# Accumulating transfers ordered behind the power, the convolution's mean moved one branch earlier, and the feed-forward reloads in pairs

## The chip, the cores and the metric

The kernel runs on one core of one Trainium2 chip. The metric is the device time of one execution in microseconds (us), the median of several runs. TensorE is called PE here, VectorE DVE, ScalarE ACT, GpSimd POOL and SyncE SP; each has its own queue of instructions and takes them strictly in order.

## What is computed

Two layers of a hybrid encoder over 1024 positions of 1024 channels, float32 in and out. Cut to what matters here:

```python
for l in range(2):
    h = rmsnorm(x, attn_norm_g[l])
    z = h @ w_in[l] + b_in[l]                       # 1024 -> 6912 channels
    a = zc_left * sigmoid(zc_right)                 # branch 0: convolution
    a = silu(layernorm(dwconv_causal(a, conv_w)))   #   31 taps per channel
    u, v = gelu(zg)                                 # branch 1: gated MLP
    sv = blockwise(ws, layernorm(v)) + bs           #   chunks of 128 positions
    p = multiscale_pool(zp, pool_w, pool_scale)     # branch 2: pooling
    y = g0*(a @ conv_proj) + g1*((u*sv) @ gmlp_proj) + g2*(p @ pool_proj)
    x = x + y @ w_out[l]
    h = rmsnorm(x, ffn_norm_g[l])
    h = dwconv_causal(h @ w_up[l], ffn_conv_w[l])   # 3 taps
    x = x + (gelu(h_left) * h_right) @ w_down[l]
return rmsnorm(x, final_norm_g)
```

## The kernel before

Everything lies transposed: 128 channels on the partitions, positions along the free axis, in two halves of 512. Each float32 operand of a matrix product is kept as a rounded part and a remainder, and a product of two operands is three matmuls (rounded by rounded, rounded by remainder, remainder by rounded). The weights of a product are loaded by SP (tiles `raw`, five buffers) and split on the way: ACT casts the rounded part, DVE subtracts it to get the remainder (`split`, L281 and L282), three operands ahead of their use. Of the three matmuls on one operand the first two read only ACT's part of the weights, the third reads DVE's.

The large input products (`IN_BLOCKS`: blocks `glu`, `v`, `zp`, `u`, `gate`, and the 16 `up` blocks of the feed-forward part) use a seven-product scheme over two by two blocks: a block is `first()` (two raw operands), `second()` (the sum s2) and `rest()` (s3, s1, one raw operand, s4), twelve matmuls of 128x512 to a product and half. The sums s1 to s4 of weight quarters are made by transfers: `begin` (L208) loads one quarter by SP, and `more` (L211 to L214) adds others by accumulating transfers on POOL's queue. The pool of these tiles has eight buffers (`s`), which the gate reloads `gt` and the tiles `uf` of the gated MLP use too. The first four blocks of a phase (`EARLY`) run on one half of the positions (operands `B`) while the other half is normalised, and then on the other (operands `T`).

The normalisation of a half goes through `rsqrt_sums` (L404 and on): PE sums squares (`st`), DVE makes `var` (L416), POOL raises it to the power -1/2 (`rs`, L418), DVE makes `rp` and the diagonal `dg` (L420 to L426), and PE spreads it over the partitions (`r`, L439). POOL has little else to compute; its queue is filled by the accumulating transfers, a memset of a part of `ws` that needs the load of `ws` to have landed (L527, L528), and in the feed-forward part the last three stores `hd` (L951).

Work that isn't the products' own is held by generators in a list `background`, and `pump(n)` runs n steps of it at places in the loops, with `PUMP = (1.4, 3, 5)` for the input blocks, branch 2 and branch 1: the 30 taps of each convolution tile (`conv_taps`, L583, one store of the tile to DRAM at its end, L588, and the sum `csum` of all tiles), the pooling windows, the gated MLP's spatial product (`spatial`: reloads v and u, the products `sv`, then `svf` and `us`), and `conv_norm`: it reloads `csum` and the six convolved tiles (`convn`), subtracts the mean, sums squares, then normalises and applies silu.

After the input blocks of a layer come the pooling product (`mix`, 84 matmuls in the order of the tiles, on `pooled_0` to `pooled_5`, of which the last three are reloaded at its start), branch 2 (`ph_2_k` on `mixed`), branch 1 (`ph_1_k` on `us`) and branch 0 (`ph_0_k` on `a`), eight tiles k of 36 matmuls each, the output product in two halves, and the feed-forward part. There the 16 results `h` go to DRAM, and half 0 and half 1 of them are reloaded for the two passes of `down` (`pd`). In `down(0)` all of half 1 is reloaded at once after tile 1 (`acts_of(1)`).

A scheduler of the framework sets the order on each engine from the program; dependences are semaphores. `tc.issue_after(ins)` adds an edge, so that what is issued inside stands behind `ins`.

Of the kernel before, what the change touches and what calls it, by code (L numbers as in the profile page):

```python
# [11 lines left out]
ALU = mybir.AluOpType  # L12
# [5 lines left out]
H = 512  # L18
NH = S // H
DB = 768  # L20
# [15 lines left out]
N_SLOTS, N_TT, N_S, N_RAW, N_SPLIT = 37, 6, 8, 5, 5  # L36
PUMP = (1.4, 3, 5)
WU = 1024
# [62 lines left out]
def encoder(ctx: ExitStack, tc: tile.TileContext, xt, wts, par, bs, wst, cnt, out):  # L101
# [82 lines left out]
    raws, sums, split = {}, {}, {}  # L184
    state = {"raw": 0, "split": 0, "used": 0, "dma": None, "credit": 0}

# [24 lines left out]
    def more(s, *others):  # L211
        for o in others:
            nc.gpsimd.dma_start(s, o, accum_op=ALU.add)  # L213
        return s  # L214
# [93 lines left out]
    def pump(n):  # L308

        state["credit"] = state["credit"] + n if background else 0  # L310
        while state["credit"] >= 1 and background:
            job = background.pop(0)
            try:
                next(job)
                state["credit"] -= 1
                background.insert(1, job)
            except StopIteration:
                pass
# [87 lines left out]
    def rsqrt_sums(ss, c0, nc_, n, name):  # L406
# [10 lines left out]
        rs = sm.tile([P, NB], F32, tag="rs", name=f"rs_{name}")  # L417
        nc.gpsimd.tensor_tensor(rs[:, :nb], var[:, :nb], mhalf[:, :nb], op=ALU.pow)  # L418
        rp = sm.tile([P, 2, NB], F32R, tag="rp", name=f"rp_{name}")
# [139 lines left out]
    def mixer_in(l, x0, x1, sq1, ops):  # L559
# [94 lines left out]
        def block(n):  # L654
            kind, j = IN_BLOCKS[n]
            return Block(l, *in_tiles(kind, j), ops, f"{kind}_{tag}_{j}")
# [29 lines left out]
        for n in range(len(IN_BLOCKS)):  # L686
            if n >= EARLY:
                b = block(n)
                b.first()
                if n == len(IN_BLOCKS) - 1:  # L690
                    for _ in range(3):
                        load_pooled(l, d)
                pump(PUMP[0])
                b.second()
                pump(PUMP[0])
            else:
                b = blocks[n]
            rest(n, b, PUMP[0])
            if n == 4:
                load_constants(l)  # L700
# [11 lines left out]
    def mixer_out(l, d, x_src, x_dst):  # L712
# [96 lines left out]

        def conv_norm():  # L810
            conv = []
            acc = wide(f"csum_{tag}_b")
# [6 lines left out]
            for h in range(NH):  # L819
# [4 lines left out]
                for i in range(KB):  # L824
# [9 lines left out]
                    yield  # L834
                dg = rsqrt_sums(sq, 0, H, DB, f"c_{tag}_{h}")
                yield
# [43 lines left out]
        for h in range(NH):  # L880
            background.insert(h, spatial(h))
        branch(2, mixed, PUMP[1])
        drain()
# [35 lines left out]
    def ffn(l, x0, x1, sq1, ops, x_src, x_dst):  # L919
# [35 lines left out]
        def load_h(i, h):  # L955
            u = slot(f"h_{tag}_{i}_{h}")
            reload(whole_of(u), hd[i][:, half(h)])
            return u
# [5 lines left out]

        def acts_of(h):
            hh = []
            for i in range(KF):
                if h == 0 and i < len(early):
                    hh.append(early[i])
                elif h == 0 and i in kept:  # L970
                    hh.append(kept[i])
                else:
                    hh.append(load_h(i, h))
                    halves_of(hh[i])
            return hh
# [18 lines left out]
        def down(h, hh, xq, khs, cols, hook, store, sq, hook_at=0):  # L994
            for m in range(KD):
# [9 lines left out]
                if store:  # L1005
                    if x_dst is not None:
                        nc.sync.dma_start(x_dst[:, m, half(h)], xm)
                    sq = square(sq, xq, m, cols, f"n_{l}_{h}_{cols.start}")
                if m == hook_at and hook is not None:
                    hook()  # L1010
            return sq

        whole, left, right = slice(0, H), slice(0, H // 2), slice(H // 2, H)
        hh0 = acts_of(0)
        x0 = x_load(x_src, 0, f"d_{l}_0")
        hh = []
        sq0 = down(0, hh0, x0, (0, 1), whole, lambda: hh.extend(acts_of(1)), True, None, 1)
        x1 = x_load(x_src, 1, f"d_{l}_1")
# [149 lines left out]
```

## Time and profile before

| what | value |
|---|---|
| median of 3 runs | 2766.7 us (2764.8 to 2769.24) |
| profiled execution, its time | 2768.68 us |
| profiled execution, its span | 2766.8 us |
| PE busy | 2691.0 us, 97% |
| DVE busy | 2058.6 us, 74% |
| ACT busy | 1254.2 us, 45% |
| POOL busy | 361.0 us, 13% |
| moved by transfers | 517.92 MB, 187 GB/s |

The profiled execution lies 2.0 us above the median. A busy share is a mean over the whole span: an engine at 74% can be full in one stage and idle in the next. Timelines below give start, length, engine, line, operation, tiles and count, and behind it in brackets the idle time of that engine just before and what ended it. Lines that begin with SPq are transfers issued by SP.

### The profile page before, as it was taken

The numbers are of one execution on the slowest core, as the hardware profiler recorded it, in microseconds if no ns is written. First come the engines' busy times: TensorE is split into PE (matmuls) and PEld (weight loads), VectorE is DVE, ScalarE is ACT, GpSimd is POOL, SyncE is SP. The second block draws the span as 40 slices with busy tenths as digits, with TensorE's granted clock in tenths as the row PEclk, the third lists the DMA queues.
The fourth block names the chain that finished last, engine by engine and source line by source line (L and its number), as shares of the span: only waits on it lengthen the run. The fifth ranks groups of instructions, "written<-read, shape, count | busy, mean of one in ns | idle before, by whom it ended". The sixth has DMA issues, their size and how long they took to land.

```text
span 2766.8 us, 35058 instructions
## 1 busy us (share of the span) xinstructions
PE 2691.0 (97%) x12122; PEld 2214.3 (80%) x12122; DVE 2058.6 (74%) x2899; ACT 1254.2 (45%) x2059; POOL 361.0 (13%) x411
## 2 busy tenths in 40 slices
PE   5999999999999999999999999999999999999998
PEld 3887888888788788877888878888877887888788
DVE  6979879786856876664579779797867569666746
ACT  4644444442423554453355444444433336445534
POOL 2212111100010121110012121110000102211000
PEclk9999999999999999999999999999999999999999
DMA  8777787675366587786358877876643847774644
GB/s 227 179 198 191 212 235 193 187 275 175 100 173 223 146 210 174 182 231 203 118 126 202 208 200 206 223 196 202 226 142 126 248 148 182 196 178 123 233 155 138
DMA packets 272003, 517.92 MB, mean 187 GB/s; under 512 B 28496, under 2 KB 49744, under 8 KB 271824
## 3 DMA queue, kind: packets, MB, share of 16 engines
q1 hardware_dynamic: 217200, 415.51, 45.2%
q0 software_dynamic: 54624, 100.16, 21.8%
q8 instruction: 95, 1.56, 0.2%
q14 instruction: 84, 0.69, 0.1%
HBM read 385.54 MB, written 89.13 MB: 172 GB/s over the span
## 4 chain that ended last, share of the span: by engine, by line
PE 87%; DVE 6%; DMA 3%; issue 2%; ACT 1%; POOL 1%; SPq 0%; DVEq 0%; POOLq 0%; ACTq 0%
PE ph L331 13%; PE run_up L331 12%; PE pd L331 11%; PE c_up L331 9%; PE run_gate L331 9%; PE c_gate L331 7%; PE po L331 6%; PE run_glu L331 4%; PE c_glu L331 3%; PE run_v L331 2%; DVE conv L583 2%; PE run_zp L331 2%; PE c_v L331 2%; PE run_u L331 1%; PE c_zp L331 1%
## 5 line engine op out<-in xcount | busy, mean ns | idle before, releaser
L282 DVE TENSOR_TENSOR split<-raw,split 128x512 fp32r<-128x512 f32 (+1 forms) x570 | 376.6, 665 | 268.4 <-ACT split L281 265.6
L281 ACT CAST split<-raw 128x512 fp32r<-128x512 f32 (+1 forms) x570 | 341.6, 602 | 459.9 <-PE pd L331 178.7
L583 DVE SCALAR_TENSOR_TENSOR conv<-z_glu,par,conv 128x1023 f32<-128x1023 f32 (+9 forms) x360 | 452.0, 1263 | 10.0 <-ACT conv L581 7.8
L281 ACT CAST split<-s 128x512 fp32r<-128x512 f32 x344 | 213.4, 622 | 356.5 <-issue 117.1
L331 PE MATMUL pd<-h,split 128*128 128x512 f32 (+1 forms) x1536 | 316.6, 365 | 7.3 <-ACT split L281 4.2
L331 PEld LDWEIGHTS pd<-h,split 128*128 128x128 f32 x1536 | 263.0, 190 | 56.5 <-ACT split L281 5.5
L213 POOL DMA_DIRECT2D s<-in_wts_dram x220 | 206.1, 957 | 711.7 <-DMA s<-in_wts_dram 406.5
L282 DVE TENSOR_TENSOR split<-s,split 128x512 fp32r<-128x512 f32 x344 | 235.1, 686 | 76.7 <-ACT split L281 76.2
L213 POOL DMA_DIRECT2D s<-s x156 | 135.7, 870 | 767.2 <-DMA s<-in_wts_dram 367.3
L331 PE MATMUL run_up<-T_f,split 128*128 128x512 f32 x768 | 184.5, 390 | 2.5 <-ACT T_f L340 2.5
L331 PE MATMUL run_up<-B_f,split 128*128 128x512 f32 x768 | 183.3, 393 | 2.5 <-DVE upv L357 2.5
L331 PE MATMUL c_up<-T_f,split 128*128 128x512 f32 x768 | 183.8, 389 | 0.3 <-ACT p_up L393 0.3
L331 PE MATMUL po<-y,split 128*128 128x512 f32 x768 | 175.7, 389 | 0.0
L331 PEld LDWEIGHTS run_up<-B_f,split 128*128 128x128 f32 x768 | 144.2, 189 | 34.7 <-DVE upv L357 4.7
L331 PEld LDWEIGHTS run_up<-T_f,split 128*128 128x128 f32 x768 | 143.8, 188 | 33.5 <-ACT T_f L340 3.3
L331 PEld LDWEIGHTS c_up<-T_f,split 128*128 128x128 f32 x768 | 144.0, 188 | 31.0 <-ACT p_up L393 1.2
L331 PEld LDWEIGHTS po<-y,split 128*128 128x128 f32 x768 | 144.0, 188 | 29.8
L331 PE MATMUL ph<-us,split 128*128 128x512 f32 x576 | 141.6, 404 | 9.9 <-DVE split L282 9.9
L331 PEld LDWEIGHTS ph<-us,split 128*128 128x128 f32 x576 | 110.6, 194 | 37.9 <-DVE split L282 12.4
L331 PE MATMUL run_gate<-T_m,split 128*128 128x512 f32 x576 | 138.3, 389 | 0.0
L331 PE MATMUL c_gate<-T_m,split 128*128 128x512 f32 x576 | 138.3, 389 | 0.0
L331 PE MATMUL run_gate<-B_m,split 128*128 128x512 f32 x576 | 135.7, 389 | 0.0
(256 smaller groups left out, 4413.8 us busy)
## 6 DMA issues: line engine op xcount, KB each, us to landing
raw<-in_wts_dram SPq DMA_DIRECT2D x518, 256.0 KB, 3.5
s<-in_wts_dram SPq DMA_DIRECT2D x344, 256.0 KB, 3.6
s<-in_wts_dram POOLq DMA_DIRECT2D x220, 256.0 KB, 5.6
s<-s POOLq DMA_DIRECT2D x156, 256.0 KB, 4.1
gate<-z_gate SPq DMA_DIRECT2D x48, 512.0 KB, 4.1
gt<-gate SPq DMA_DIRECT2D x96, 256.0 KB, 3.6
h<-hd SPq DMA_DIRECT2D x56, 256.0 KB, 5.6
poold<-pooled SPq DMA_DIRECT2D x24, 512.0 KB, 4.5
```

The costliest lines, as they stand in the source:

```text
L213: nc.gpsimd.dma_start(s, o, accum_op=ALU.add)
L281: nc.scalar.copy(s[:, 0, :cols], src[:, :cols])
L282: nc.vector.tensor_tensor(s[:, 1, :cols], src[:, :cols], s[:, 0, :cols].bitcast(F32), op=ALU.subtract)
L331: nc.tensor.matmul(ps[:, cols], w[:, i0, wsl], a[:, i1, cols], start=first and k == 0 and j == 0, stop=last and k == n - 1 and j == 2, ski ...
L583: nc.vector.scalar_tensor_tensor(acc[:, k:], ain[:, : S - k], col(w0 - k), acc[:, k:], op0=ALU.mult, op1=ALU.add,)
```

## The change

Seven edits in the program.

- `rsqrt_sums` notes its power instruction in `state["pow"]`, and `more` issues the accumulating transfers behind the last one noted.
- `PUMP` becomes (1.4, 5, 5), so branch 2 runs five background steps per half tile.
- `LAST_PUMP = 1.8` replaces 1.4 in the last six input blocks.
- `conv_norm` is cut in two. `conv_mean` (reloads, mean, subtraction, squares) is appended to the background before branch 2, `conv_norm` (power, normalisation, silu) stays before branch 1.
- `acts_of(1)` goes; `first_acts` does what it did for half 0.
- `two_more` reloads two tiles of half 1 per call.
- `down` calls its hook after every tile if `hook_at` is None, as it is now for half 0.

```diff
-PUMP = (1.4, 3, 5)
+PUMP = (1.4, 5, 5)
+LAST_PUMP = 1.8
...
     def more(s, *others):
-        for o in others:
-            nc.gpsimd.dma_start(s, o, accum_op=ALU.add)
+
+        with ExitStack() as order:
+            if state["pow"] is not None:
+                order.enter_context(tc.issue_after(state["pow"]))
+            for o in others:
+                nc.gpsimd.dma_start(s, o, accum_op=ALU.add)
         return s
...
-        nc.gpsimd.tensor_tensor(rs[:, :nb], var[:, :nb], mhalf[:, :nb], op=ALU.pow)
+        state["pow"] = nc.gpsimd.tensor_tensor(
+            rs[:, :nb], var[:, :nb], mhalf[:, :nb], op=ALU.pow
+        ).ins
...
+                rate = PUMP[0] if n < len(IN_BLOCKS) - 6 else LAST_PUMP
                 b = block(n)
                 b.first()
...
-                pump(PUMP[0])
+                pump(rate)
                 b.second()
-                pump(PUMP[0])
+                pump(rate)
...
-        def conv_norm():
-            conv = []
+        conv, squares = [], []
+
+        def conv_mean():
             acc = wide(f"csum_{tag}_b")
...
+                squares.append(sq)
+
+        def conv_norm():
+            for h in range(NH):
+                sl = half(h)
+                dg = rsqrt_sums(squares[h], 0, H, DB, f"c_{tag}_{h}")
                 yield
...
+        background.append(conv_mean())
         branch(2, mixed, PUMP[1])
         drain()
         background.append(conv_norm())
...
-                if m == hook_at and hook is not None:
+                if hook is not None and hook_at in (m, None):
                     hook()
...
-        sq0 = down(0, hh0, x0, (0, 1), whole, lambda: hh.extend(acts_of(1)), True, None, 1)
+
+        def two_more():
+            for i in range(len(hh), min(len(hh) + 2, KF)):
+                hh.append(load_h(i, 1))
+                halves_of(hh[i])
+
+        sq0 = down(0, hh0, x0, (0, 1), whole, two_more, True, None, None)
```

What the scheduler makes of it is seen in the order of instructions. First POOL's queue at the start of layer 0, from the second transfer onto each of the first four s2 sums on; `s_0_1_409` to `_413` and `s_0_12_540` are the sums s1, s3 and s4 of the first blocks. Before:

```order
L213 DMA s_0_14_272<-in_wts_dram 128x512
L213 DMA s_0_24_276<-in_wts_dram 128x512
L213 DMA s_0_1_409<-in_wts_dram 128x512
L213 DMA s_0_1_411<-in_wts_dram 128x512
L213 DMA s_0_1_413<-in_wts_dram 128x512
L213 DMA s_0_1_413<-s_0_1_409 128x512
L213 DMA s_0_12_540<-in_wts_dram 128x512
L528 MEMSET ws_1208 64x4x64
L418 TENSOR_TENSOR rs_m_1_378<-var_m_1_376,mhalf 128x4
```

After:

```order
L218 DMA s_0_14_272<-in_wts_dram 128x512
L218 DMA s_0_24_276<-in_wts_dram 128x512
L535 MEMSET ws_1208 64x4x64
L423 TENSOR_TENSOR rs_m_1_378<-var_m_1_376,mhalf 128x4
L218 DMA s_0_1_409<-in_wts_dram 128x512
L218 DMA s_0_1_411<-in_wts_dram 128x512
L218 DMA s_0_1_413<-in_wts_dram 128x512
L218 DMA s_0_12_540<-in_wts_dram 128x512
L218 DMA s_0_12_542<-in_wts_dram 128x512
```

Five transfers went from ahead of the power to behind it; the memset of `ws` still stands ahead of it. The same edge moves the eight s2 transfers of the feed-forward part's first blocks behind the power of its half 0, and those of layer 1 behind the power of layer 1's half 0, with the three stores `hd` now ahead of them.

Second SP's queue in the pooling product of layer 0 (`convd` is the store of the last convolution tile, `poold` the pooled tiles in DRAM). Before:

```order
L682 DMA gate_22_239<-z_gate_11_4519 128x1024
L192 DMA raw_4854<-in_wts_dram 128x256
L200 DMA pooled_3_0_b<-poold_3_259 128x1024
L200 DMA pooled_3_1_b<-poold_3_259 128x1024
L200 DMA pooled_4_0_b<-poold_4_260 128x1024
L200 DMA pooled_4_1_b<-poold_4_260 128x1024
```

After:

```order
L689 DMA gate_22_239<-z_gate_11_4604 128x1024
L193 DMA raw_4869<-in_wts_dram 128x256
L595 DMA convd_5_246<-conv_5_4314 128x1024
L201 DMA pooled_3_0_b<-poold_3_259 128x1024
L201 DMA pooled_3_1_b<-poold_3_259 128x1024
L201 DMA pooled_4_0_b<-poold_4_260 128x1024
```

The store of the convolution's last tile went from 31 rows behind the last of the six pooled loads to just ahead of the first. On DVE the taps of that tile begin one gate block earlier, and its last tap stands between the second and the third `mixed` tile of the pooling product. The reloads `csum_b` and `convn` stand in the middle of branch 2, the two `mean` matmuls in tile 4 of branch 2, and the gated MLP's `sv` products begin behind 54 matmuls of branch 2 (in the middle of tile 1), where they began behind 90 (in the middle of tile 2).

Third DVE's queue in branch 1 of layer 0, up to the next remainder of branch 1's weights after the second half's `r_c`. Before, the last eleven rows of twenty-two:

```order
L870 TENSOR_TENSOR gt_1_3_0_5892<-ph_1_3_0_5894,gt_1_3_0_5892 128x512
L870 TENSOR_TENSOR gt_1_3_1_5915<-ph_1_3_1_5917,gt_1_3_1_5915 128x512
L341 TENSOR_TENSOR a_1_2_5832<-convn_2_5557,a_1_2_5832 128x512
L848 TENSOR_TENSOR convn_3_5559<-convn_3_5559,csg_1_3_5836 128x512
L357 TENSOR_TENSOR yacc_3_4846<-yacc_3_4846,gt_1_3_0_5892 128x512
L848 TENSOR_TENSOR convn_4_5561<-convn_4_5561,csg_1_4_5867 128x512
L357 TENSOR_TENSOR yacc_3_4846<-yacc_3_4846,gt_1_3_1_5915 128x512
L341 TENSOR_TENSOR a_1_3_5840<-convn_3_5559,a_1_3_5840 128x512
L848 TENSOR_TENSOR convn_5_5563<-convn_5_5563,csg_1_5_5875 128x512
L341 TENSOR_TENSOR a_1_4_5871<-convn_4_5561,a_1_4_5871 128x512
L282 TENSOR_TENSOR split_5938<-raw_5885,split_5938 128x256
```

After, all thirteen but the first (`convn_0` by `r_c_1`):

```order
L855 TENSOR_TENSOR convn_1_5252<-convn_1_5252,r_c_1_5719 128x512
L855 TENSOR_TENSOR convn_2_5254<-convn_2_5254,r_c_1_5719 128x512
L855 TENSOR_TENSOR convn_3_5256<-convn_3_5256,r_c_1_5719 128x512
L855 TENSOR_TENSOR convn_4_5258<-convn_4_5258,r_c_1_5719 128x512
L863 TENSOR_TENSOR convn_0_5250<-convn_0_5250,csg_1_0_5723 128x512
L863 TENSOR_TENSOR convn_1_5252<-convn_1_5252,csg_1_1_5731 128x512
L855 TENSOR_TENSOR convn_5_5260<-convn_5_5260,r_c_1_5719 128x512
L346 TENSOR_TENSOR a_1_0_5727<-convn_0_5250,a_1_0_5727 128x512
L346 TENSOR_TENSOR a_1_1_5735<-convn_1_5252,a_1_1_5735 128x512
L863 TENSOR_TENSOR convn_2_5254<-convn_2_5254,csg_1_2_5772 128x512
L885 TENSOR_TENSOR gt_1_1_1_5803<-ph_1_1_1_5805,gt_1_1_1_5803 128x512
L287 TENSOR_TENSOR split_5826<-raw_5741,split_5826 128x256
```

The next remainder now stands behind twelve instructions instead of twenty-one, and PE's queue holds 37 matmuls from the second half of `r_c_1` to the first that reads it (38 before).

In the feed-forward part SP's queue now has two reloads `h` of half 1 between groups of four weight loads, where 16 stood together.

## Rows read from the trace of the kernel before

**Rows 1.** The page, the chain of work that ended last: share of the span by engine.

```profile
PE 87%; DVE 6%; DMA 3%; issue 2%; ACT 1%; POOL 1%; SPq 0%; DVEq 0%; POOLq 0%; ACTq 0%
```

**Rows 2.** The waits of PE over the whole span: who waited for whom, us in total, times, the longest.

```profile
PE r_m L439 <- DVE dg_m L426: 13.0, 2, 10.3
PE ph L331 <- DVE split L282: 9.9, 4, 4.7
PE pd L331 <- ACT split L281: 4.2, 3, 2.7
PE run_up L331 <- DVE upv L357: 2.5, 2, 1.9
...
PE mix L331 <- DMA pooled_b<-poold: 0.3, 1, 0.3
```

**Rows 3.** POOL's timeline at the start of layer 0.

```profile
42.75 0.86 POOL L213 DMA_DIRECT2D s<-in_wts_dram  x1 [1.20 <-issue]
50.33 0.88 POOL L213 DMA_DIRECT2D s<-s  x1 [6.72 <-DMA s<-in_wts_dram]
...
52.16 0.31 POOL L528 MEMSET ws<- 64x256 f32 x1
52.55 1.04 POOL L418 TENSOR_TENSOR rs_m<-var_m,mhalf 128x4 f32<-128x4 f32 x1
```

**Rows 4.** PE's timeline in the same stretch; `run_glu<-T_m` is the first product on the other half.

```profile
41.45 2.91 PE L331 MATMUL c_v<-B_m,split 128*128 128x512 f32 x12
54.64 1.40 PE L439 MATMUL r_m<-dg_m,ones_r 128*128 128x512 f32 x2 [10.28 <-DVE dg_m L426]
...
65.59 0.50 PE L331 MATMUL run_glu<-T_m,split 128*128 128x512 f32 x1 [1.74 <-ACT T_m L340]
```

**Rows 5.** DVE's timeline in the same stretch.

```profile
53.62 0.17 DVE L420 CAST rp_m<-rs_m 128x4 fp32r<-128x4 f32 x1 [12.01 <-POOL rs_m L418]
...
63.52 0.69 DVE L357 TENSOR_TENSOR z_zp<-c_zp,p_zp 128x512 f32<-128x512 f32 x1 [2.10 <-PE c_zp L331]
```

**Rows 6.** The load of `ws`: SP's timeline, and from the transfers issued between 28 and 50 us the line with size and us to landing.

```profile
34.28 0.67 SPq L527 DMA_DIRECT2D ws<-in_wst_dram  x1
...
ws<-in_wst_dram SPq DMA_DIRECT2D x1, 256.0 KB, 10.0
```

**Rows 7.** PE's timeline at the end of the up blocks and in `down(0)` of layer 0.

```profile
1204.88 2.88 PE L331 MATMUL run_up<-T_f,split 128*128 128x512 f32 x12
1207.60 2.88 PE L331 MATMUL c_up<-T_f,split 128*128 128x512 f32 x12
1212.34 3.99 PE L331 MATMUL run_up<-B_f,split 128*128 128x512 f32 x11 [1.86 <-DVE upv L357]
...
1258.20 6.00 PE L331 MATMUL pd<-h,split 128*128 128x512 f32 x18 [2.74 <-ACT split L281]
```

**Rows 8.** The waits of PE between 2550 and 2610 us, the same place in layer 1: the line of the up block.

```profile
PE run_up L331 <- DVE upv L357: 0.6, 1, 0.6
```

**Rows 9.** SP's timeline in `down(0)` of layer 0.

```profile
1243.93 6.55 SPq L200 DMA_DIRECT2D h<-hd  x11
1250.83 2.34 SPq L192 DMA_DIRECT2D raw<-in_wts_dram  x4
```

**Rows 10.** DVE's timeline in branch 1 of layer 0, from the first instruction on the second half's `r_c`.

```profile
717.10 3.08 DVE L840 TENSOR_TENSOR convn<-convn,r_c 128x512 f32<-128x512 f32 x5
720.15 1.40 DVE L848 TENSOR_TENSOR convn<-convn,csg 128x512 f32<-128x512 f32 x2
721.47 0.68 DVE L840 TENSOR_TENSOR convn<-convn,r_c 128x512 f32<-128x512 f32 x1
722.07 1.30 DVE L341 TENSOR_TENSOR a<-convn,a 128x512 fp32r<-128x512 f32 x2
...
730.17 0.42 DVE L282 TENSOR_TENSOR split<-raw,split 128x256 fp32r<-128x256 f32 x1
```

**Rows 11.** PE's timeline in the same stretch.

```profile
716.90 9.09 PE L331 MATMUL ph<-us,split 128*128 128x512 f32 x38
730.64 9.73 PE L331 MATMUL ph<-us,split 128*128 128x512 f32 x31 [4.65 <-DVE split L282]
```

**Rows 12.** The stretch of 10 us after that wait: length, then busy time and count of PE, PE's weight loads, DVE, ACT and POOL, then PE's granted clock as a share of 2.4 GHz, the transfers' share and GB/s.

```profile
730.00:740.00 10.00, 9.36 (x31) 7.50 (x32) 9.60 (x18) 1.02 (x2) 0.00 (x0) 0.71 0.67 212
```

**Rows 13.** The pooling product of layer 0: from the timelines of SP, PE and DVE (two lines), and for the tiles `pooled_b` the us from issue to landing of its six loads.

```profile
579.17 2.93 SPq L200 DMA_DIRECT2D pooled_b<-poold  x6
...
574.88 19.11 PE L331 MATMUL mix<-pooled_b,split 128*128 128x512 f32 x83
...
577.33 0.75 DVE L748 SCALAR_TENSOR_TENSOR mixed<-mix,par,mixed 128x512 fp32r<-128x512 f32 x1
...
579.25 1.26 DVE L583 SCALAR_TENSOR_TENSOR conv<-z_glu,par,conv 128x1005 f32<-128x1005 f32 x1
...
DMA to landing us min/median/max: 4.3/6.3/9.6
```

**Rows 14.** Branch 2 of layer 0: the last of eight scalings of `v` on ACT and the first `sv` products on PE, and from the page the line of the gate stores (KB each, median us to landing).

```profile
610.92 1.03 ACT L775 ACTIVATE v<-v,nm,rv 128x768 f32<-128x768 f32 x1
...
614.23 2.97 PE L786 MATMUL sv<-ws,v 128*128 128x128 f32 x32
...
gate<-z_gate SPq DMA_DIRECT2D x48, 512.0 KB, 4.1
```

More of the change, by code (lines that the diff above doesn't have):

```diff
@@ L184, in encoder @@
     raws, sums, split = {}, {}, {}
-    state = {"raw": 0, "split": 0, "used": 0, "dma": None, "credit": 0}
+    state = {"raw": 0, "split": 0, "used": 0, "dma": None, "credit": 0, "pow": None}
     def load_to(n):
@@ L692, in mixer_in @@
                         load_pooled(l, d)
-                pump(PUMP[0])
+                pump(rate)
                 b.second()
-                pump(PUMP[0])
+                pump(rate)
             else:
-                b = blocks[n]
-            rest(n, b, PUMP[0])
+                b, rate = blocks[n], PUMP[0]
+            rest(n, b, rate)
             if n == 4:
@@ L834, in conv_norm @@
                     yield
-                dg = rsqrt_sums(sq, 0, H, DB, f"c_{tag}_{h}")
+                squares.append(sq)
[3 more added lines that the diff above has]
+                dg = rsqrt_sums(squares[h], 0, H, DB, f"c_{tag}_{h}")
                 yield
@@ L963, in splits, with first_acts @@
                 yield
-        def acts_of(h):
+        def first_acts():
             hh = []
             for i in range(KF):
-                if h == 0 and i < len(early):
+                if i < len(early):
                     hh.append(early[i])
-                elif h == 0 and i in kept:
+                elif i in kept:
                     hh.append(kept[i])
                 else:
-                    hh.append(load_h(i, h))
+                    hh.append(load_h(i, 0))
                     halves_of(hh[i])
@@ L1013, in ffn @@
         whole, left, right = slice(0, H), slice(0, H // 2), slice(H // 2, H)
-        hh0 = acts_of(0)
+        hh0 = first_acts()
         x0 = x_load(x_src, 0, f"d_{l}_0")
         hh = []
-        sq0 = down(0, hh0, x0, (0, 1), whole, lambda: hh.extend(acts_of(1)), True, None, 1)
+        def two_more():
[3 more added lines that the diff above has]
+        sq0 = down(0, hh0, x0, (0, 1), whole, two_more, True, None, None)
         x1 = x_load(x_src, 1, f"d_{l}_1")
```

## The prediction

> **What bounds the kernel now.** I read the page first. The chain of work that ended last lies on PE for 87% of the span, and the rest of it is the moments at which PE waits for DVE, a transfer or ACT [rows 1]. So an edit counts only where PE stands still, or where its clock falls because it stood still. The second view is therefore the list of PE's waits [rows 2], and the third the timelines around each wait. Four of them lie where this change works: r_m at the start (10.3 us), ph in branch 1 (9.9 us in four waits, that is about 4.95 us a layer), pd in down(0) of layer 0 (2.7) and run_up just ahead of it (1.9). The pace of PE at full clock is 12 matmuls in 1207.60 - 1204.88 = 2.72 us, 0.227 us each [rows 7]; slower stretches are priced against that.
>
> A wait has a tail. After the wait of 4.65 us the granted clock of the next 10 us is 0.71, that is 5.8 us at 1.2 GHz and 4.2 us at 2.4 GHz, and 10 x 0.29 = 2.9 us lost [rows 11, 12]. After the 2.74 us in down(0), 18 matmuls took 6.00 us where 18 x 0.227 = 4.1 is the pace, or 4.25 with the last one's overhang: 1.75 us lost. After the 1.86 us, 11 took 3.99 instead of 2.5: 1.5 us lost [rows 7].
>
> **The power, at the start.** POOL's power begins at 52.55 and r_m on PE at 54.64, 2.1 us later; DVE had waited 12 us for it [rows 3 to 5]. What stood ahead of the power on POOL is an accumulating transfer from one sum to another, for which POOL's queue waited 6.7 us until 50.33 [rows 3]. That transfer and four others go behind the power. One instruction stays ahead, the memset of ws, and it needs the load of ws: issued at 34.28, 10.0 us to landing, so 44.3 [rows 6]. From the memset's start to the power's start are 0.4 us [rows 3]: power at 44.7, r_m at 46.8, which is 7.8 us sooner. PE has just finished c_v then (41.45 + 2.91 = 44.4 [rows 4]), so its pause is 2.4 us instead of 10.3. In the present run DVE also waits 2.1 us on c_zp, the product behind r_m [rows 5]; PE with less of a pause should run that in time, and the first product on the other half (65.59 [rows 4]) hangs on DVE. I take 7.8 + 2.1, rounded to **-10**. Bounds: -12.4 if ws lands early enough that only c_v holds r_m (54.64 - 44.36 = 10.3, and 2.1); -6 if ws lands 2 us later and the 2.1 don't come back. The transfers behind the power are needed only in the second round of products on the other half; nothing else is queued behind the power on POOL.
>
> The load of ws ran beside POOL's accumulating transfers, and after the change there is nothing on POOL's queue from the last s2 sum to the power. The Trainium skill, DMA: Bandwidth & Descriptors, section "Queues, rings and completion order", says that each of the 16 engines goes round the queues that have work for it, packet by packet. By that rule ws lands sooner when POOL's queue is empty, and this term moves towards -12.4; no row here shows ws alone, so the sum doesn't use it.
>
> **The sums of the other phases.** In layer 0's feed-forward part the transfers for layer 1 move behind layer 1's first power, and the product that needs them comes later still. The wait of 1.86 us at 1212 stands where DVE and ACT work on reloaded tiles; in layer 1, where no next layer's sums are loaded, the same wait is 0.6 [rows 7, 8]. I take the difference, 1.3, and the 1.5 us of slow matmuls: **-2.8** (0 if the reloads are late for another reason, to -3.4).
>
> **Reloads in pairs.** Eleven reloads stand together on SP from 1243.93 on, weight loads behind them only at 1250.83 [rows 9], and PE waits 2.74 us for the cast of a weight at 1258.20 [rows 7]. With two reloads between groups of four weight loads that queue goes. The wait and its tail are 4.5; I keep 0.5 for the small waits that ACT's casts may leave: **-4.0** (0 to -4.5). In layer 1 I count on nothing: this wait is 2.7 of the 4.2 us that pd waits for casts in all [rows 2].
>
> **Branch 1, per layer.** Before, DVE starts on the second half's r_c at 717.10 and comes to the next remainder of a weight at 730.17, 13 us later, while PE had 38 matmuls, 9.1 us, and then stood 4.65 us [rows 10, 11]. Now DVE has twelve instructions ahead of that remainder. The same twelve took from 717.10 to 723.4 for the first ten (five, two, one, two), and two more of 0.6 make 7.3; with the remainder's 0.42 it is 7.7 us [rows 10]. PE has 37 matmuls in its queue, 8.4 us. So the wait ends. The 4.95 us of waits and the 2.9 of clock are 7.8; I leave 1 us for waits on dg: **-6.8 a layer** (-3 if ACT's share of the same chain holds DVE up, to -7.8).
>
> **The pooling product, per layer.** Six pooled loads are issued from 579.17 on; the first lands 4.3 us later at 583.5, the last (issued at 581.6) 9.6 us later, so they land 1.5 us apart [rows 13]. PE reads the fourth pooled tile after 42 of 84 matmuls, at 574.88 + 42 x 0.226 = 584.4: 0.9 us of slack, and in layer 1 none (PE already waits 0.3 [rows 2]). Now the store of the last convolution tile stands ahead of them on SP and waits for the last tap. That tap follows the second mixed tile. The first mixed tile starts at 577.33 and one tap takes 1.2 us [rows 13], so mixed, tap, mixed, tap end at 577.3 + 0.7 + 1.2 + 0.7 + 1.2 = 581.1, and the loads are issued 2.1 us later. The store is as large as one of the loads, another 1.5 us if it goes ahead of them. Landing 3.6 us later with 0.9 of slack makes 2.7, and 0.5 more because the second tile lands 1.5 us behind the first and is wanted 0.7 behind it: 3.2, and with a part of a tail such as 1.75 I take **+4 a layer** (+1.2 if the store holds up none of the loads' bytes, +5 with a full tail).
>
> The Trainium skill, DMA: Bandwidth & Descriptors, section "Queues, rings and completion order", says that each engine takes the descriptors of one ring in order, so a store that SP issues first is served first. This speaks against the change: by it the mix costs 3.2 and the tail, without it 1.2. No row shows a store just ahead of a load that PE waits for.
>
> **Branch 2, per layer.** Twelve subtractions, ten additions and the spatial product come earlier into branch 2. The sv products begin 36 matmuls, 8.2 us, sooner than 614.23, at 606.0, while the last scaled v was ready at 610.92 + 1.03 = 612 [rows 14]; the order gives PE 18 other matmuls (4.1 us) to run between, and the later mix moves PE by some 3 us more. That leaves 0 to 5; I take **+1**. The taps moved earlier fill two gate blocks of DVE to about 19 us of 19, as some blocks are now without a wait: 0.
>
> **The sum.** -10 - 2.8 - 4.0 + 2 x (-6.8 + 4 + 1) = -20.4. From the profiled execution's 2768.7 that is 2748.3; the median stands 2.0 us below that execution, so **2746**.
>
> **The rivals.**
> 1. *The store lets the loads by.* Mix +1.2, branch 2 at 0, the other terms as they are at their good ends: -12.4 - 3.4 - 4.5 + 2 x (-7.8 + 1.2) = -33.5, giving 2733. For it: stores and loads move in opposite directions; against: six loads that land 1.5 us apart show transfers queueing for bandwidth already.
> 2. *The power does not get ahead.* If ws lands only when the accumulating transfers would have been done, the first term is 0: -10.4, 2756. Against it: ws landed at 44.3 with those transfers beside it.
> 3. *The moved work makes as many waits as it takes away.* Mix and branch 2 at +5 each, branch 1 at -3: +7 a layer, -16.8 + 14 = -2.8, 2764.
> 4. *Slower: the mean.* Its matmul stands in PE's queue in tile 4 of branch 2, and everything behind it waits for csum: last spatial work on DVE, sum, store (4.1 us for 512 KB [rows 14]), reload. From the end of tile 2 PE has 65 matmuls to the mean, 14.7 us; DVE has four instructions of about 0.6 and the sum of 1.2, then the store and a reload of the same size, an estimate of 3.6 + 4.1 + 4.1 = 11.8: it just fits. Each us that DVE is later than the 2.9 left costs one in each layer. From a wait of 7.3 us, with a tail of 2.9, the two layers lose 20.4 and the change is no gain; at a wait of 11 us it is 2 x 13.9 - 20.4 = +7.4, so 2774. Against it: that needs DVE 14 us, nearly two tiles, behind PE.
>
> **How the numbers follow.** The forecast has 0.60 (its own range 2738 to 2755), rival 1 0.15, rival 2 0.08, rival 3 0.11, rival 4 0.06. The range that leaves out two in ten is 2732 to 2762. A measurement of this kernel can tell about 0.2% from no change, 5.5 us: faster is below 2761.2, slower above 2772.2. Faster: forecast, rivals 1 and 2, 0.83. Same: rival 3, 0.11. Slower: 0.06.
>
> **What would show it.** POOL's power at 44 to 45 and r_m near 47 show the first term right; r_m above 50 shows it wrong. A wait of mix for pooled_b of about 3 us in both layers, with a granted clock below 1 behind it, shows the store; none shows rival 1. No ph wait for a split above 1 us in branch 1, and no pd wait for a split near 1255, show the steps on branch 1 and on the reloads. A wait of mean or sv in branch 2 of over 3 us would make the prediction wrong, and so would up blocks that wait as long as now.

## The result, and the profile after

The changed kernel takes **2744.3 us** (median of 4, 2742.2 to 2748.5), against 2768.0 us for the kernel before in the same measurement (4 executions, 2764.8 to 2770.6): a ratio of 0.9917, interval 0.99 to 0.9934. 2746 was predicted. The profiled execution took 2748.52 us with a span of 2746.8 us, the highest of the four; it stands 20.2 us below the profiled one of before, where the working had -20.4.

That the sum agrees hides that its terms don't all. This table compares the start of each stage's first matmul on PE in the two traces. In both layers one product of 12 matmuls (2.72 us) changed places with the start of the pooling product; it is counted where it stood before.

| stage | forecast, us | trace after minus before, us |
|---|---|---|
| start to the first product on the other half | -10 | -10.2 |
| rest of the input blocks, layer 0 / 1 | 0 | +1.5 / -0.8 |
| pooling product, layer 0 / 1 | +4 each | +4.2 / +4.8 |
| branch 2, layer 0 / 1 | +1 each | +1.9 / +6.7 |
| branch 1, layer 0 / 1 | -6.8 each | -10.3 / -10.2 |
| up blocks, layer 0 / 1 | -2.8 / 0 | -1.6 / +0.1 |
| `down`, layer 0 / 1 | -4.0 / 0 | -4.5 / -1.8 |
| all | -20.4 | -20.1 |

The waits of PE over the whole span (who waited for whom; us in total, times, the longest), to be laid beside [rows 2]:

```profile
PE mix L336 <- DMA pooled_b<-poold: 3.9, 3, 3.2
...
PE r_m L446 <- DVE dg_m L433: 2.8, 1, 2.8
PE mean L832 <- DMA csum_b<-csumd: 2.7, 1, 2.7
...
PE run_up L336 <- DVE upv L362: 2.3, 2, 1.6
PE mix L336 <- DVE mixed L757: 2.1, 1, 2.1
...
PE pd L336 <- ACT split L286: 1.5, 2, 0.8
```

The 10.3 us of r_m (the 2.8 left are layer 1's) and the 9.9 us of ph for a split are gone. The line of mean is new, mix waits 3.9 us for the pooled loads where it waited 0.3, and 2.1 us of mix are put down to DVE. run_up has stayed.

POOL at the start, beside [rows 3]: the memset of `ws` comes when the load lands, the power 0.4 us behind it, and the accumulating transfers behind the power.

```profile
43.72 0.31 POOL L535 MEMSET ws<- 64x256 f32 x1 [8.53 <-DMA ws<-in_wst_dram]
44.11 1.04 POOL L423 TENSOR_TENSOR rs_m<-var_m,mhalf 128x4 f32<-128x4 f32 x1
45.11 2.71 POOL L218 DMA_DIRECT2D s<-in_wts_dram  x3
```

PE there, beside [rows 4]: r_m starts as c_v ends (43.19 + 2.91 = 46.10), and the first product on the other half at 55.37 instead of 65.59. The product between them, run_zp, took 2.90 us; its line from the trace of before comes first.

```profile
55.84 4.82 PE L331 MATMUL run_zp<-B_m,split 128*128 128x512 f32 x12
```

```profile
43.19 2.91 PE L336 MATMUL c_v<-B_m,split 128*128 128x512 f32 x12
46.20 1.10 PE L446 MATMUL r_m<-dg_m,ones_r 128*128 128x512 f32 x2
47.14 2.90 PE L336 MATMUL run_zp<-B_m,split 128*128 128x512 f32 x12
...
55.37 0.50 PE L336 MATMUL run_glu<-T_m,split 128*128 128x512 f32 x1 [2.16 <-ACT T_m L345]
```

DVE in branch 1 of layer 0, beside [rows 10]: from the first instruction on the second half's r_c to the next remainder of a weight are 702.22 - 694.60 = 7.6 us, where they were 730.17 - 717.10 = 13.1. PE shows no wait from 668.7 to 737.6.

```profile
694.60 3.08 DVE L855 TENSOR_TENSOR convn<-convn,r_c 128x512 f32<-128x512 f32 x5
...
702.22 0.41 DVE L287 TENSOR_TENSOR split<-raw,split 128x256 fp32r<-128x256 f32 x1
```

The pooling product of layer 0, beside [rows 13]: DVE's first `mixed`, SP's store and six loads, then PE.

```profile
568.16 0.75 DVE L757 SCALAR_TENSOR_TENSOR mixed<-mix,par,mixed 128x512 fp32r<-128x512 f32 x1
```

```profile
571.92 0.32 SPq L595 DMA_DIRECT2D convd<-conv  x1
572.33 3.61 SPq L201 DMA_DIRECT2D pooled_b<-poold  x6
```

```profile
565.87 9.68 PE L336 MATMUL mix<-pooled_b,split 128*128 128x512 f32 x42
577.67 0.93 PE L336 MATMUL mix<-pooled_b,split 128*128 128x512 f32 x3 [2.12 <-DVE mixed L757]
578.94 10.55 PE L336 MATMUL mix<-pooled_b,split 128*128 128x512 f32 x39 [0.33 <-DMA pooled_b<-poold]
```

PE stands still after the 42 matmuls that need no fourth pooled tile. Here the trace names DVE as the releaser: the first of two `mixed` that begin at 576.89 ends at 577.6. But the first of the six loads took 5.2 us to land, so 572.33 + 5.2 = 577.5, and the two can't be told apart by time in this trace. Experiment 4 settles that it was the load. In layer 1 the same wait is 3.19 us and named the load's, as it is in layer 0 of experiments 1, 3, 5 and 8 (2.4 to 2.9 us). The next view shows what followed.

Stretches of after: in layer 0 the 5 us with the wait and the next 5 us, in layer 1 the 5 us behind the wait, then the 5 us in which the mean's wait ends (length; busy time and count of PE, its weight loads, DVE, ACT, POOL; granted clock; transfers' share; GB/s):

```profile
575.00:580.00 5.00, 2.55 (x9) 1.52 (x8) 2.01 (x3) 1.78 (x3) 0.00 (x0) 0.86 0.95 338
580.00:585.00 5.00, 5.00 (x19) 4.02 (x18) 0.75 (x1) 0.92 (x2) 0.00 (x0) 0.80 1.03 402
...
1926.00:1931.00 5.00, 4.63 (x14) 3.40 (x13) 0.00 (x0) 0.00 (x0) 0.00 (x0) 0.66 1.03 410
...
1990.00:1995.00 5.00, 2.75 (x4) 1.21 (x5) 0.64 (x1) 0.00 (x0) 0.00 (x0) 0.67 1.00 382
```

The mean of layer 1: DVE's sum, then SP's store and reload of `csum`, then PE.

```profile
1980.09 1.22 DVE L362 TENSOR_TENSOR csum<-csum,conv 128x1024 f32<-128x1024 f32 x1
```

```profile
1981.82 0.38 SPq L604 DMA_DIRECT2D csumd<-csum  x1
...
1986.31 0.33 SPq L201 DMA_DIRECT2D csum_b<-csumd  x1
```

```profile
1970.47 19.09 PE L336 MATMUL ph<-mixed,split 128*128 128x512 f32 x83
1992.25 3.41 PE L832 MATMUL mean<-csum_b,ones 128*128 128x512 f32 x4 [2.69 <-DMA csum_b<-csumd]
```

The reload is issued 4.5 us behind the store and lands 5.9 us later, at 1992.2. That is 10.4 us from the store to the mean, where the working had 8.2. In layer 0 the mean doesn't wait: its reload lands 3.9 us after the issue, at 640.7, and the product ahead of it ends then.

```profile
631.40 1.22 DVE L362 TENSOR_TENSOR csum<-csum,conv 128x1024 f32<-128x1024 f32 x1
```

```profile
636.84 0.33 SPq L201 DMA_DIRECT2D csum_b<-csumd  x1
```

```profile
621.78 19.09 PE L336 MATMUL ph<-mixed,split 128*128 128x512 f32 x83
640.78 1.98 PE L832 MATMUL mean<-csum_b,ones 128*128 128x512 f32 x4
```

The end of the up blocks, beside [rows 7], with a wait almost as long as before, but no slow matmuls behind it:

```profile
1199.29 3.02 PE L336 MATMUL run_up<-B_f,split 128*128 128x512 f32 x12 [1.63 <-DVE upv L362]
```

### The profile page after: what moved, and what is told of

Read it like the earlier page. It is cut to its first block, busy times and chain, and to the rows that moved or that the text cites. A ratio compares the mean times of both kernels' runs of the same rounds, so it can differ in the third digit from the quotient of the medians.

```text
span 2746.8 us, 35054 instructions
## 1 busy us (share of the span) xinstructions
PE 2682.3 (98%) x12122; PEld 2209.9 (80%) x12122; DVE 2057.0 (75%) x2899; ACT 1255.1 (46%) x2059; POOL 359.1 (13%) x411
## 4 chain that ended last, share of the span: by engine, by line
PE 80%; issue 7%; DVE 6%; DMA 4%; ACT 1%; POOL 0%; SPq 0%; DVEq 0%; POOLq 0%; ACTq 0%
PE run_up L336 12%; PE pd L336 12%; PE run_gate L336 10%; PE c_up L336 9%; PE ph L336 9%; PE c_gate L336 7%; PE po L336 4%; PE run_glu L336 4%; PE c_glu L336 3%; DVE conv L590 2%; PE run_v L336 2%; PE c_v L336 2%; PE run_zp L336 1%; DMA poold<-pooled 1%; PE mix L336 1%
## 5 line engine op out<-in xcount | busy, mean ns | idle before, releaser
L590 DVE SCALAR_TENSOR_TENSOR conv<-z_glu,par,conv 128x1023 f32<-128x1023 f32 (+9 forms) x360 | 451.8, 1262 | 10.4 <-ACT conv L588 8.3
L336 PE MATMUL ph<-mixed,split 128*128 128x512 f32 x576 | 135.3, 393 | 0.0
L336 PE MATMUL ph<-us,split 128*128 128x512 f32 x576 | 134.2, 391 | 0.0
```

Source lines behind the costliest of these rows:

```text
L336: nc.tensor.matmul(ps[:, cols], w[:, i0, wsl], a[:, i1, cols], start=first and k == 0 and j == 0, stop=last and k == n - 1 and j == 2, ski ...
L590: nc.vector.scalar_tensor_tensor(acc[:, k:], ain[:, : S - k], col(w0 - k), acc[:, k:], op0=ALU.mult, op1=ALU.add,)
```

## The experiments

Each starts from the changed kernel and was compared with the kernel before on the same chip, so the ratios, not the times, are to be laid beside the changed kernel's 0.9917 (0.99 to 0.9934).

**1. No order behind the power.**

```diff
-            if state["pow"] is not None:
-                order.enter_context(tc.issue_after(state["pow"]))
```

> The changed kernel (2744 us) without the ordering edge: the accumulating transfers go to POOL as the kernel before has them, all else stays changed. Theory (each term sits where the two traces differ): the first product on the other half starts 10.2 us later again, near 65.6, and the up blocks of layer 0 lose 1.6 us again, so 2744 + 12 = 2756. Rival (the order also thins out the transfers elsewhere, for all reloads): more than 16 us slower, 2760 and above, with losses spread over both layers. Second rival (only the start counts): 2744 + 10 = 2754 and the wait at the last up block as in the changed kernel, 1.6 us, with no slow matmuls behind it.

2755.2 us (2754.5 to 2757.2), 0.9945 (0.993 to 0.996), by the ratios 7.8 us above the changed kernel. PE waits for r_m again, 10.0 us:

```profile
54.06 1.40 PE L443 MATMUL r_m<-dg_m,ones_r 128*128 128x512 f32 x2 [9.99 <-DVE dg_m L430]
```

The stage at the start is 10.1 us longer than with the order, so the first term is the order's, whole. But the up blocks of layer 0 are as fast as with it (-1.6 us against before, both times), as the second rival said: in this trace their gain came without the order. Experiment 5 takes that up.

**2. The convolution part as before**: mean and normalisation in one generator before branch 1, `PUMP` (1.4, 3, 5), no `LAST_PUMP`.

```diff
-PUMP = (1.4, 5, 5)
+PUMP = (1.4, 3, 5)
...
-        background.append(conv_mean())
         branch(2, mixed, PUMP[1])
```

> The changed kernel with the convolution's part put back: mean, squares and normalisation all in branch 1, pump rates 1.4, 3 and 5. By the two profiled executions the pooling product then gains 4.2 and 4.8 us, branch 2 gains 1.9 and 6.7, branch 1 loses 10.3 and 10.2: net +2.9, so 2747. Rival (the profiled execution of the changed kernel lies 4 us above its median, and the surplus sits in the waits for the mean and the pooled tiles, which vary from run to run): +6 or more, 2750 and above.

2748.6 us (2745.8 to 2750.8), 0.9922 (0.9905 to 0.994). Branch 1 is 10.0 and 9.3 us longer than in the changed kernel; shorter by as much together are the rest of the input blocks (2.3 and 1.3 us), the pooling product (3.7 and 4.5) and branch 2 (1.9 and 6.7; the exchanged product is set right as above). The ratios can't be told apart: **the part of the change that takes 20 us off branch 1 brings nothing on balance that these runs can tell from zero**, -1.4 us by the ratios. The working had -3.6. The input blocks' share is no firm figure: experiment 3, which has the earlier taps too, is only 0.2 and 0.3 us longer there than this run.

**3. The reloads at once.** All 16 after tile 1 of `down(0)`.

```diff
-        sq0 = down(0, hh0, x0, (0, 1), whole, two_more, True, None, None)
+        def all_more():
+            for _ in range(KF // 2):
+                two_more()
+
+        sq0 = down(0, hh0, x0, (0, 1), whole, all_more, True, None, 1)
```

> The changed kernel with the 16 reloads of half 1 issued together after tile 1 of down(0), as before. Theory: the wait of 2.7 us near 1240 in layer 0 and its slow matmuls come back, 4.5 us, and the 1.7 us that the down part of layer 1 gained go too: 2744 + 6 = 2750. Rival (layer 1's gain is not of the reloads): 2744 + 4.5 = 2748 or 2749, layer 1's down part as in the changed kernel. Second rival (the burst is harmless once the sums are out of the way): 2744.

2750.9 us (2749.3 to 2753.0), 0.9929 (0.9913 to 0.9944). Against the changed kernel's trace `down` is 4.7 us longer in layer 0 and 1.9 us in layer 1; the ratios are 3.3 us apart, with intervals that meet. And the wait for a weight's cast is back, as the list of waits shows:

```profile
PE pd L336 <- ACT split L286: 4.1, 3, 2.6
```

**4. The store of the last convolution tile behind the weight loads and the pooled loads.**

```diff
-            nc.sync.dma_start(d["conv"][i], acc)
+            (nc.sync.dma_start if i < KB - 1 else reload)(d["conv"][i], acc)
```

> The changed kernel with one edge more: the store of the last convolution tile goes behind the weight load that was issued last in the program, so SP issues it behind the pooled loads. Theory (the store that waits for the last tap delays the pooled loads): the waits of mix, 2.4 us in layer 0 and 3.6 in layer 1, and their slow matmuls go, -4 a layer, 2736. Rival (the pooled loads are late for their buffers or for bandwidth): no change, 2744. Rival for layer 0 alone, where the trace names DVE's mixed tile as the releaser: its 2.1 us stay and only layer 1 gains, 2740.

2737.0 us (2732.6 to 2741.8), 0.9878 (0.986 to 0.9897). Mix waits 1.5 us in four waits, none over 0.5, and its stage is 3.3 and 4.3 us shorter. Both layers gain, and the trace settles what held PE in layer 0:

```profile
573.54 0.92 PE L336 MATMUL mix<-pooled_b,split 128*128 128x512 f32 x3 [0.31 <-DMA pooled_b<-poold]
```

PE goes on at 573.54, 1.0 us before the two `mixed` begin (574.58), and these begin 11.0 us behind the start of the pooling product, as in the changed kernel. So DVE did not hold PE there; the load did. The six loads are issued 0.5 us behind the start of the first `mixed`, where they were issued 4.2 us behind it (568.16 to 572.33), but the first takes 7.0 us to land instead of 5.2: issued 3.6 us sooner, it lands 1.8 us sooner.

**5. The order at the start alone**: `state["pow"]` is set for names that begin with `m_0`.

```diff
+        if name.startswith("m_0"):
+            state["pow"] = power
```

> The order behind the power is kept for the first normalisation of layer 0 alone; the transfers of the feed-forward part's first blocks and of layer 1 go back to where they stood. Theory: the run without any order lost only at the start (T_m), the up blocks' gain came to both, so the other orders are worth nothing: 2744, as the changed kernel. Rival: the other orders are worth the 1.6 to 2.8 us that the up blocks gained: 2746 to 2747.

2746.4 us (2739.9 to 2747.7), 0.9929 (0.9912 to 0.9946). By the ratios it is 3.3 us above the changed kernel, where the rival puts it, but the interval holds the theory too. In its trace the up blocks of layer 0 are 2.1 us longer than in the changed kernel's: the wait at their end is 2.14 us, and slow matmuls are back behind it.

```profile
1197.69 4.61 PE L336 MATMUL run_up<-B_f,split 128*128 128x512 f32 x12 [2.14 <-DVE upv L362]
```

That wait differs from trace to trace. Over all twelve, with its length and the time of the 12 matmuls behind it in layer 0, then the wait in layer 1:

| kernel | wait, layer 0 | 12 matmuls | wait, layer 1 |
|---|---|---|---|
| before | 1.86 | 4.41 | 0.59 |
| after | 1.63 | 3.02 | 0.72 |
| 1, no order | 1.51 | 3.06 | 0.93 |
| 2, old convolution part | 0.95 | 3.01 | 0.31 |
| 3, reloads at once | 1.67 | 3.02 | 0.82 |
| 4, store behind | 1.51 | 3.01 | 1.28 |
| 5, order at the start | 2.14 | 4.61 | 0.29 |
| 6, sum ahead (below) | 1.12 | 3.02 | 0.59 |
| 6, the same with the store behind | 1.86 | 3.04 | 0.63 |
| 7, small store | 0.71 | 3.01 | 1.68 |
| 8, sum ahead, paced | 1.83 | 3.02 | 0.71 |
| 9, the same with the store behind | 0.80 | 3.02 | 1.17 |

The order at this place is missing in before, 1 and 5 (1.51 to 2.14 us, slow matmuls in two of three) and present in the other nine (0.71 to 1.86 us, slow matmuls in none). So the traces lean towards the order, but the two ranges meet and 1 has the whole gain of 1.6 us without it. Whether the order shortens this wait is not shown.

**6. The sum ahead of the spatial product, alone and with the store behind the pooled loads.** The background was emptied ahead of the spatial product's generators.

```diff
+        drain()
         for h in range(NH):
             background.insert(h, spatial(h))
```

> The last of the convolution's tiles is summed, and csum stored, ahead of the gated MLP's spatial product instead of behind it. Theory: the wait of the mean's matmuls for csum in branch 2 of layer 1 (2.7 us, with its slow clock 5 to 6 of the 6.7 us by which that stage grew) and about 1 us in layer 0 end: 2738. Rival: the reloads, subtractions and squares that now come earlier push sv's and us's work on DVE back, and new waits take the place of the old: 2744 or above.

> Both at once: the last convolution tile's store stands behind the last pooled load on SP's queue, and the sum and its store come ahead of the spatial product. Theory: the two gains add (7 for the store, 6 for the sum): 2731. Rival: they are the same time seen twice, and it is no better than the store alone: 2737.

2771.9 us (2767.3 to 2772.6), 1.002 (1.001 to 1.003), and 2762.1 us (2758.3 to 2767.4), 0.9989 (0.9979 to 0.9998). The first lies in its rival's range and the second near neither of its two, and none of the expectations named the cause. The edit did more than it meant: emptying the list adds 1000 to the credit of `pump`, and what wasn't used let all of the spatial product out at the next pump, so that `sv` began behind 18 matmuls of branch 2 instead of 54. PE in the first of the two:

```profile
589.49 4.24 PE L336 MATMUL ph<-mixed,split 128*128 128x512 f32 x18
599.21 0.79 PE L795 MATMUL sv<-ws,v 128*128 128x128 f32 x2 [5.47 <-ACT v L784]
```

Branch 2 grew by 14.5 and 9.8 us over the changed kernel. These two say nothing on the sum, and show what pacing is worth there.

**7. A small store in the same place.** The last convolution tile is stored early from the taps' input, and after the last tap only 64 of its 1024 positions, so the other convolved values of that tile are left out.

```diff
+            if i == KB - 1:
+                nc.sync.dma_start(d["conv"][i], ain)
...
-            nc.sync.dma_start(d["conv"][i], acc)
+            if i < KB - 1:
+                nc.sync.dma_start(d["conv"][i], acc)
+            else:
+                nc.sync.dma_start(d["conv"][i][:, :64], acc[:, :64])
```

> The store ahead of the pooled loads waits for the last tap as before, but carries only 64 of 1024 positions; the tile's other positions are stored earlier, from the taps' input, so that the convolved values of the last tile are left out there. It splits the price of the store between the later issue (2.1 us by the prediction) and the bytes ahead of the loads (1.5). Theory, both count: each layer's mix gains about 1.5, 2740 to 2741. Rival, only the wait for the tap counts: 2744. Rival, only the bytes count: 2737.

2739.5 us (2733.8 to 2743.1), 0.9907 (0.9888 to 0.9925). Its trace splits the price. The first of layer 0's six loads lands 4.2 us after its issue, as before the change [rows 13], instead of 5.2 us, and mix waits 1.1 us instead of 2.1, in layer 1 1.0 instead of 3.2:

```profile
574.91 0.93 PE L336 MATMUL mix<-pooled_b,split 128*128 128x512 f32 x3 [1.10 <-DMA pooled_b<-poold]
```

The clock stays at 1.00 there. The ratio can't tell the three expectations apart; the stages can. They are 2.3 and 3.7 us shorter than in the changed kernel, where moving the store away (experiment 4) brought 3.3 and 4.3. So the bytes, with the slow clock behind the longer wait, are the larger part, and the later issue is 1.0 and 0.6 us. It counts for so little because the loads that experiment 4 issues sooner take longer to land, 7.0 us for the first against 4.2 here.

**8 and 9. The sum ahead, paced**: the credit set to zero behind the emptying; in 9 the store stands behind the last pooled load too.

```diff
+        drain()
+        state["credit"] = 0
         for h in range(NH):
```

> The sum of the convolution's tiles again ahead of the spatial product, but with the background's credit set to zero behind it: emptying the background by a large pump left nearly a thousand steps of credit, and in the run before this one the whole spatial product and the mean were let out at the first pump of branch 2. Now PE's order is that of the changed kernel, and only the sum, its store and its reload stand earlier. Theory: the mean's wait for csum in layer 1 (2.7 us) and its slow clock end, branch 2 of layer 1 grows by 1 to 2 us over before as layer 0's does instead of 6.7: about 2739. Rival: the mean then waits for the six convn reloads or for DVE instead, or the slow clock has another cause: 2743 or above.

> The last convolution tile's store behind the last pooled load, and the sum ahead of the spatial product with the credit set to zero. Theory: the store alone gave 2737, with the mean's wait still there in layer 1 (2.4 us); without it, and its tail, 2732. Rival: 2737, no better than the store alone.

8 took 2743.0 us (2735.0 to 2745.3), 0.9916 (0.9903 to 0.9929), and 9 2732.7 us (2731.8 to 2739.0), 0.9886 (0.9874 to 0.9899). The order was not quite the changed kernel's: the mean stands behind 58 matmuls after the last `sv`, 25 fewer. It still doesn't wait, as PE's timeline of 8 shows at the place of the 2.69 us:

```profile
1966.02 13.43 PE L336 MATMUL ph<-mixed,split 128*128 128x512 f32 x58
1979.29 1.88 PE L832 MATMUL mean<-csum_b,ones 128*128 128x512 f32 x4
```

Branch 2 of layer 1 is 4.9 us shorter than in the changed kernel's trace, in 8 and in 9 alike. The mechanism is shown, but the time of 8 is not lower by that: its ratio is the changed kernel's. Of the five other kernels with the late sum and the mean in branch 2, the longest wait of mean was 0.9, 2.8, 2.4, 1.9 and 0.6 us (1, 3, 4, 5, 7), so the changed kernel's 2.7 us lies at the upper end of what an execution shows. In these six traces branch 2 of layer 1 is 0.8 to 5.4 us longer than in 8 and 9, 3.6 in the mean, so the usual price is less than the 4.9 us of one trace. 9 has the lowest median and is 0.3% below the changed kernel by the ratios; against 4 its ratio is no lower, so what is shown of that is the store's place.

## Why the prediction came out right

- **The power.** Right in mechanism: power forecast at 44.7, seen at 44.11; r_m at 46.8, seen at 46.20; -10 against -10.2. Experiment 1 shows that it is the order's. That the size agrees to 0.2 us is luck, as in the ten traces with this order the stage is 8.1 to 12.9 us shorter than before. The working expected a pause of 2.4 us on PE, and there is none, because c_v too ended 1.7 us later than before (46.10 against 44.36). The 2.1 us that the working put down to c_zp came mostly from the product ahead of it: run_zp took 4.82 us behind the long wait and 2.90 without it. The load of `ws` took 9.1 us to land here and 9.9 us in experiment 1, where POOL's transfers run beside it. By the Trainium skill, DMA: Bandwidth & Descriptors, section "Queues, rings and completion order", each engine goes round the queues that have work, so the load should gain from an empty POOL queue. These two traces agree, with 0.8 us between them, and so do eight of the other nine with the order (8.3 to 9.6 us); experiment 9's load took 10.1 us, so the gain is not shown.
- **The sums of the other phases.** Half of this step failed. It read the difference between layer 0's wait (1.86) and layer 1's (0.59) in one execution as the cost of the transfers. The wait stayed at 1.63 with the order, close to the sign of being wrong that the prediction itself named (up blocks that wait as long as now), and twelve traces have it between 0.71 and 2.14 in layer 0 and up to 1.68 in layer 1. What went (1.6 us) is the run of slow matmuls behind it, the step's other half; but it went in experiment 1 without the order as well. Experiment 5's ratio, with the order at the start alone, is 0.0012 higher (3 us), which lies within its interval. Whether the gain is the order's stays open.
- **Reloads in pairs.** Right: -4.0 forecast, -4.5 seen (2.4 to 4.8 us shorter in the other nine traces with the pairs), 4.7 back in experiment 3. Layer 1's gain of 1.8, 1.9 back in experiment 3, was not forecast: the step counted only the wait for a cast there. Those nine traces have layer 1 between 1.7 us shorter and 0.5 longer than before, so 1.8 is the good end of it.
- **Branch 1.** The mechanism was right (DVE's twelve instructions took 7.6 us, forecast 7.3), the size too small: -10.3 against -6.8. The term was waits 4.95 and clock 2.9 less 1 us for new waits. No new wait came (1.0); the mean's matmuls left the stage (675.36 to 675.81 and 690.27 to 690.73 on PE's timeline of before, 0.9); the clock lost 0.5 us more in the 10 us ahead of those of [rows 12], at 0.95; the small waits were 0.3 more. That makes 9.5; some 0.7 us a layer are not assigned.
- **The pooling product.** Right in place, cause and total: +4 forecast, +4.2 and +4.8. Experiment 4 shows the store as the cause, experiment 7 that both its wait for the tap and its bytes count. Their shares were not as the working had them, 2.1 us for the later issue (581.1 - 579.17 is 1.9) and 1.5 for the bytes: by the stages of experiments 4 and 7 the bytes with the slow clock are 2.3 and 3.7 us, the issue 1.0 and 0.6. So the close total is in part luck. Of rival 1 nothing is left. With the rule of the Trainium skill that the prediction draws on (DMA: Bandwidth & Descriptors, section "Queues, rings and completion order"), by which a store that SP issues first is served first, the trace agrees: 5.2 us to the first landing behind 512 KB, 4.2 behind a sixteenth of that.
- **Branch 2 and the taps.** Mis-sized: +1 a layer forecast for branch 2, +1.9 and +6.7 seen. Of it 1.4 us in layer 0 (640.78 to 642.20) are the mean's matmuls, which came from branch 1 and stand in neither term. The taps that were priced at nothing in the gate blocks cost 2.3 and 1.3 us by experiment 2, which experiment 3 doesn't bear out, so their price is not shown. Layer 1's is rival 4's mechanism at a third of the price from which it would have decided: a wait of 2.7 with a slow clock. The slack of 2.9 us was used up by DVE: from PE's end of tile 2 (18 matmuls behind 621.78 and 1970.47) to the end of the sum the working had 3.6 us, and it took 6.8 in both layers, since eight instructions, not four, and a wait of 0.8 us for ACT stood ahead of the sum. The chain from the store to the reload's landing, put at 4.1 + 4.1, then took 4.2 + 3.9 in layer 0, where the mean just didn't wait, and 4.5 + 5.9 in layer 1, where it did. Six `convn` loads stand behind the reload in both; why it lands later in layer 1 is open. Forecasting the wait as "just fits" and then pricing it at nothing was the fault; the end of a chain that just fits should have had half its range in the term.
- **The sum.** -20.4 came true as -20.2 because errors cancelled: branch 1 was 6.9 us better than forecast in the two layers, branch 2 6.6 us worse, the reloads 2.3 us better, the other terms 2.8 us worse. The median lies 4 us below the profiled execution, which the working could not know.

## What to carry to other kernels

When work is moved off a stage that waits, list the transfers that move with it: here one store, issued just ahead of the loads that the next product needs, and one sum whose store and reload end just ahead of their reader, took back more than half of the 20 us that the move won (7.6 and 4.9 us in the traces). Ordering such a store behind the loads paid here (experiment 4). Computing a sum that makes a round trip through DRAM as soon as its last part exists took its reader's wait away (8 and 9), but a lower time by it was not shown.

Don't read the difference between two places in one execution as a cause: the wait at the end of the up blocks differs by as much between traces, and twelve of them don't settle the cause. And an edit that lets a paced list run empty has to restore the pacing's state.

## What was not expected of the hardware

A wait of the same length is sometimes followed by the lower of PE's two clocks and sometimes not. At one place, the 12 matmuls behind a wait of 1.86 us took 4.41 us in before and 3.04 us in the second kernel of experiment 6, and 4.61 us behind 2.14 us. At the start, PE waited 2.01 us for r_m in the first kernel of experiment 6, and run_zp behind it took 2.90 us; in experiment 9 it waited 1.46 us, and run_zp took 4.50 us, at a granted clock of 0.69 between 47 and 52 us. In the 5 us in which mean's 2.69 us end, the granted clock was 0.67. So a wait of some 2 us can cost nearly twice its length, and its length alone does not tell whether it will.

The same 512 KB store took 2.9 us to land when SP issued it ahead of the six loads, and 10.4 us behind them (experiment 9, layer 0). PE doesn't wait for it there, so the place that is slow for the store is the cheap one.
